# A two-layer decoder trunk on one core: the order of instructions from another model of the chip

## The chip, the core and the metric

The kernel runs on one of the eight cores of a Trainium2 chip. A core has five engines that matter here, each with its own in-order queue: PE (TensorE, matrix products), ACT (ScalarE), DVE (VectorE), POOL (GpSimd) and SP (SyncE, which here only issues loads). An engine waits at the instruction at the head of its queue until that instruction's inputs and its target buffer are free; what stands behind it waits too. The metric is the device time of one execution in microseconds.

## The reference

x holds 256 tokens of 1024 features, c one vector of 1024. Two layers follow each other, and each has three sublayers: an FFN, a mixer, an FFN. Each sublayer is

```
h = rms_norm(x, pre_g) * (1 + scale) + shift
x = x + res_w * gate * rms_norm(fn(h), post_g)
```

where shift, scale and gate come from one product of c with ada_w (1024 x 9216 per layer). The functions are:

```
swiglu: a, b = split(h @ w_in);  (silu(a) * b) @ w_out            # D_FF = 2816
hgrn2:  q, f, i, g = split(h @ w_in); a gated linear recurrence over chunks
        of 64 tokens and 8 heads; rms_norm per head, times silu(g); @ w_out
gmlp:   u, v = split(gelu(h @ w_in + b)); v = layer_norm(v)
        (u * (W_s v + b_s)) @ w_out                              # 2 x 3072 wide
```

The mixer of the first layer is hgrn2, that of the second gmlp. All data are float32.

## The kernel before

**Products.** Each float32 operand is split in two parts of the type fp32r, hi (a cast) and lo (the rest), and a product is three matmuls: hi by hi, hi by lo, lo by hi (L142 to L144 for the output product into y, L291 to L294 for the first, token-major product, L328 to L336 for the units of an FFN, L418 for the very first). The matmuls of one such group are 256 or 512 columns wide.

**Weights.** All weights pass once from HBM. `next_block` takes the blocks in a fixed list; `wblock` loads each as two halves of 128 x 1024 (tile raw, four buffers, L55), ACT casts each half to hi (L119) and DVE subtracts to get lo (L120). Twelve tiles of hi or lo exist, so six blocks; a cast has to wait until the matmuls that read the tile's former content are done. Between the weight blocks `ada` loads 144 pieces of ada_w (tile ada, two buffers), and DVE reduces each against c into a column of mod (L169, an instruction and its accumulator's readout). `pace` says how many pieces go with how many blocks. All these loads are issued by SP, and `keep_in_program_order` (L55) fixes their order to that of the code.

**Stages.** In order: ffn0 (to 207 us), HGRN2 (to 382), ffn1 (to 574), ffn2 (to 770), gMLP (to 996), ffn3 (to the end). An FFN runs through units of 256 hidden columns: two products into ups, silu on ACT, a multiplication on DVE, a split into t, and the output product of an earlier unit into four accumulators y (two token tiles t = 0, 1, each with two halves of 512 columns). The last three units' output products are left for `out_last`, which the loop at the end calls for one token tile and half after the other.

**The end of a sublayer, `tail`.** For each token tile: the output product of half 0, then ACT squares y with a row sum (L216), DVE be (L218), yg = y * G (L259); half 1, squares, root on ACT (L79, named sq), reciprocal r (L224), yg (L263), and x = x + r * yg (L265, two halves). Then `prenorm`'s part for the next sublayer: squares of x (L216), be, root, r, xn = x * r (half 0 on DVE, L233; half 1 on ACT, L235), transposes on PE into npa (L239, four per half; their banks are those of y), hf = npa * A + shift (L243, four per half on ACT), and h's hi and lo on DVE (L247, L248). The next sublayer's first product (L291) reads h. Tile 0's chain and tile 1's output product are independent of each other.

**What sets the order.** The program is written as one sequence. The framework (`tile.TileContext`) takes this sequence with the dependencies between tiles and computes from them an order for each engine, using a model of how long every instruction takes. Exceptions are marked in the code: loads stay in program order, ACT functions stay behind the table load they need (`table`, `tact`), and `after` adds an order between two instructions. Nothing else binds the order of ACT, DVE and PE beyond the dependencies.

## Time and profile before

| what | value |
|---|---|
| median of 3 runs | 1191.43 us (1189.97 to 1196.67) |
| profiled execution | 1193.24 us, of which its span 1191.5 |
| mean granted TensorE clock | 0.984 of full speed |
| weight casts L119 / subtractions L120 | 376 each, mean 1050 / 1220 ns |
| ada reductions L169 | 144, mean 1221 ns |
| bytes read from HBM | 280.11 MB, 236 GB/s over the span |

The span runs from the first to the last recorded instruction. A row of the timeline reads: start in us, busy us, engine, line, operation, output and inputs, shape, count; in brackets the idle time of the engine ahead of it and what ended it. A row of the groups reads: line, engine, operation, operands, count, then busy us and mean ns of one, then idle us before them with what ended most of it. A row of the waits reads: engine, waiting operation, what it waited for, then us in total, times and the longest.

### The profile page before, as it was taken

The numbers are of one execution on the slowest core, as the hardware profiler recorded it, in microseconds if no ns is written. First come the engines' busy times: TensorE is split into PE (matmuls) and PEld (weight loads), VectorE is DVE, ScalarE is ACT, GpSimd is POOL, SyncE is SP. The second block draws the span as 40 slices with busy tenths as digits, with TensorE's granted clock in tenths as the row PEclk, the third lists the DMA queues.
The fourth block names the chain that finished last, engine by engine and source line by source line (L and its number), as shares of the span: only waits on it lengthen the run. The fifth ranks groups of instructions, "written<-read, shape, count | busy, mean of one in ns | idle before, by whom it ended". The sixth has DMA issues, their size and how long they took to land.

```text
span 1191.5 us, 17180 instructions
## 1 busy us (share of the span) xinstructions
PE 1146.5 (96%) x6518; PEld 995.4 (84%) x6518; DVE 888.8 (75%) x1331; ACT 657.2 (55%) x1054; POOL 6.8 (1%) x16
## 2 busy tenths in 40 slices
PE   7999999997997999999999999999999999999997
PEld 6999998797895788888778888888888887888886
DVE  6997888868887887787677787657978786666652
ACT  6464446648766754456655545554754457555541
POOL 0000000000000000000000000000000000000000
PEclk9999999997999999999999999999999999999999
DMA  9899998782335777887578888537777765666640
GB/s 345 311 314 318 333 327 314 251 285 101 124 95 185 263 267 272 278 272 262 173 251 267 282 269 272 188 124 261 277 254 262 248 212 177 203 222 233 213 137 36
DMA packets 79765, 282.32 MB, mean 237 GB/s; under 512 B 9873, under 2 KB 10561, under 8 KB 79682
## 3 DMA queue, kind: packets, MB, share of 16 engines
q1 hardware_dynamic: 78626, 278.05, 68.0%
q0 software_dynamic: 1056, 3.17, 0.8%
q8 instruction: 51, 0.84, 0.3%
q14 instruction: 32, 0.26, 0.1%
HBM read 280.11 MB, written 1.07 MB: 236 GB/s over the span
## 4 chain that ended last, share of the span: by engine, by line
PE 73%; DMA 10%; DVE 8%; ACT 5%; issue 3%; SPq 0%; DVEq 0%; ACTq 0%
PE ups L328 15%; PE ups L329 8%; PE y L144 7%; PE y L142 7%; PE y L143 7%; PE ups L418 4%; DMA ada<-in_ada 4%; DMA raw<-in_wffn 4%; DVE w L120 3%; PE ups L334 3%; PE ups L336 3%; PE ups L335 3%; DMA raw<-in_whg 3%; ACT w L119 2%; PE ab L599 2%
## 5 line engine op out<-in xcount | busy, mean ns | idle before, releaser
L120 DVE TENSOR_TENSOR w<-raw,w 128x1024 fp32r<-128x1024 f32 x376 | 453.5, 1220 | 84.7 <-ACT w L119 77.5
L119 ACT CAST w<-raw 128x1024 fp32r<-128x1024 f32 x376 | 388.0, 1050 | 202.9 <-DMA raw<-in_wffn 79.4
L328 PE MATMUL ups<-h,w 128*128 128x512 f32 x864 | 303.1, 394 | 0.0
L169 DVE CUSTOM_DVE_ANT_0 junkv<-ada,cond 128x1024 bf16<-128x1024 f32 x144 | 175.8, 1221 | 92.0 <-DMA ada<-in_ada 91.5
L329 PE MATMUL ups<-h,w 128*128 128x256 f32 x864 | 242.5, 281 | 0.0
L328 PEld LDWEIGHTS ups<-h,w 128*128 128x128 f32 x864 | 162.3, 188 | 36.8
L142 PE MATMUL y<-w,t 128*128 128x512 f32 x448 | 179.4, 400 | 4.5 <-ACT t L147 4.5
L143 PE MATMUL y<-w,t 128*128 128x512 f32 x448 | 178.2, 398 | 0.0
L144 PE MATMUL y<-w,t 128*128 128x512 f32 x448 | 177.6, 397 | 0.2
L329 PEld LDWEIGHTS ups<-h,w 128*128 128x128 f32 x864 | 163.7, 190 | 0.9
L334 PE MATMUL ups<-h,w 128*128 128x256 f32 x416 | 118.3, 285 | 0.6 <-ACT w L119 0.6
L336 PE MATMUL ups<-h,w 128*128 128x256 f32 x416 | 117.8, 283 | 0.2 <-DVE w L120 0.2
L335 PE MATMUL ups<-h,w 128*128 128x256 f32 x416 | 117.6, 283 | 0.0
L142 PEld LDWEIGHTS y<-w,t 128*128 128x128 f32 x448 | 84.5, 189 | 24.1 <-ACT t L147 5.3
L144 PEld LDWEIGHTS y<-w,t 128*128 128x128 f32 x448 | 84.3, 189 | 21.0 <-DVE t L148 1.1
L143 PEld LDWEIGHTS y<-w,t 128*128 128x128 f32 x448 | 84.5, 189 | 17.9
L79 ACT ACTIVATE t<-t 128x256 f32<-128x256 f32 (+2 forms) x70 | 36.3, 523 | 97.7 <-DVE t L378 95.5
L334 PEld LDWEIGHTS ups<-h,w 128*128 128x128 f32 x416 | 79.7, 192 | 1.7 <-ACT w L119 0.8
L335 PEld LDWEIGHTS ups<-h,w 128*128 128x128 f32 x416 | 79.7, 192 | 0.8 <-issue 0.2
L336 PEld LDWEIGHTS ups<-h,w 128*128 128x128 f32 x416 | 79.7, 192 | 0.4 <-DVE w L120 0.4
L291 PE MATMUL pps<-w,h 128*128 128x512 f32 x160 | 64.4, 403 | 5.3 <-DVE h L247 5.3
L292 PE MATMUL pps<-w,h 128*128 128x512 f32 x160 | 63.8, 399 | 0.0
(199 smaller groups left out, 1435.4 us busy)
## 6 DMA issues: line engine op xcount, KB each, us to landing
raw<-in_wffn SPq DMA_DIRECT2D x264, 512.0 KB, 5.5
ada<-in_ada SPq DMA_DIRECT2D x144, 512.0 KB, 6.5
raw<-in_wgmu SPq DMA_DIRECT2D x48, 512.0 KB, 5.2
raw<-in_whg SPq DMA_DIRECT2D x40, 512.0 KB, 5.8
raw<-in_wgmv SPq DMA_DIRECT2D x24, 512.0 KB, 5.0
G<-gflat POOLq DMA_DIRECT2D x6, 512.0 KB, 5.9
t<-in_gbin SPq DMA_DIRECT2D x6, 256.0 KB, 5.2
x<-in_x SPq DMA_DIRECT2D x2, 512.0 KB, 4.0
```

What stands on the lines that cost most here:

```text
L119: nc.scalar.copy(hi[:, sl], raw)
L120: nc.vector.tensor_sub(lo[:, sl], raw, hi[:, sl])
L142: self.paced(mm(ps, l[0], r[0], start=start, stop=False))
L143: mm(ps, l[0], r[1], start=False, stop=False)
L144: mm(ps, l[1], r[0], start=False, stop=stop)
L169: nc.vector.tensor_tensor_reduce(junk, t, self.cond, 1.0, 0.0, ALU.mult, ALU.add, self.mod[i // 24][:, i % 24:i % 24 + 1])
L291: mm(res[g][t], h(0, kc), u(0, kc), start=kc == 0, stop=False)
L328: self.paced(mm(ps, u[0], self.h2[:, :, :, kc, :], start=kc == 0, stop=False))
L329: mm(ps[:, 1, :], u[1], self.h2[:, 0, :, kc, :], start=False, stop=kc == KC - 1)
L334: self.paced(mm(o, u[0], h[0], start=start, stop=False))
L335: mm(o, u[0], h[1], start=False, stop=False)
L336: mm(o, u[1], h[0], start=False, stop=stop)
```

## The change

One argument of the framework's context is set. With it the order of each engine is computed with the tool chain's timeline model, in place of its default model of an instruction's duration. No instruction, tile, buffer or load is changed, and the sequence of the code is the same.

```
--- before.py
+++ after.py
@@ -1088,7 +1088,7 @@
-    with tile.TileContext(nc) as tc:
+    with tile.TileContext(nc, schedule_with_timeline_sim=True) as tc:
         with ExitStack() as ctx:
             Body(ctx, tc, args, out).run()
```

SP's and POOL's orders are the same as before. On PE, DVE and ACT the order differs in many places. Three are shown. A name with a number is one tile: x_99 is x of tile 0 and x_100 of tile 1; `x2` is a row that comes twice.

*First place: DVE at the end of ffn0, from the update of x of tile 0 to xn.* y_799 and y_800 are the two halves of tile 1's output. Before:

```order
L265 SCALAR_TENSOR_TENSOR x_99<-yg,r,x_99 128x512 x2
L120 TENSOR_TENSOR w<-raw,w 128x1024
L218 TENSOR_SCALAR be<-s_2156 128x1
L120 TENSOR_TENSOR w<-raw,w 128x1024
L224 RECIPROCAL r<-sq 128x1
L169 ISA junkv,mod_104<-ada,cond 128x1024
L169 ISA mod_104 128x1
L233 TENSOR_SCALAR xn<-x_99,r 128x512
```

and now:

```order
L218 TENSOR_SCALAR be<-s_2156 128x1
L169 ISA junkv,mod_105<-ada,cond 128x1024
L169 ISA mod_105 128x1
L169 ISA junkv,mod_105<-ada,cond 128x1024
L169 ISA mod_105 128x1
L120 TENSOR_TENSOR w<-raw,w 128x1024 x2
L224 RECIPROCAL r<-sq 128x1
L218 TENSOR_SCALAR be<-s_2214 128x1
L259 TENSOR_TENSOR yg<-y_799,G 128x512
L120 TENSOR_TENSOR w<-raw,w 128x1024
L263 TENSOR_TENSOR yg<-y_800,G 128x512
L233 TENSOR_SCALAR xn<-x_99,r 128x512
```

Between x of tile 0 and xn there were two weight subtractions and one ada reduction; now there are three and two, and both halves of tile 1's yg, so that xn stands behind the end of y_800. After xn come, now, two more subtractions, two ada reductions and the update of x_100 ahead of the first L247; before, it was L259, an ada reduction and a subtraction.

*Second place: PE at the end of gMLP.* y_7904 and y_7905 are tile 0's halves, y_7906 and y_7907 tile 1's. Before:

```order
L142 MATMUL y_7907<-w,t_9058 128x512
L143 MATMUL y_7907<-w,t_9058 128x512
L144 MATMUL y_7907<-w,t_9058 128x512
L239 MATMUL npa<-ident,xn 128x128 x4
L142 MATMUL y_7907<-w,t_9058 128x512
L143 MATMUL y_7907<-w,t_9058 128x512
L239 MATMUL npa<-ident,xn 128x128 x4
L144 MATMUL y_7907<-w,t_9058 128x512
L142 MATMUL y_7907<-w,t_9140 128x512
```

and now:

```order
L144 MATMUL y_7906<-w,t_9161 128x512
L144 MATMUL y_7907<-w,t_9161 128x512
L142 MATMUL y_7907<-w,t_9161 128x512
L143 MATMUL y_7907<-w,t_9161 128x512
L144 MATMUL y_7907<-w,t_9161 128x512
L239 MATMUL npa<-ident,xn 128x128 x8
L291 MATMUL pps<-w,h_9339 128x512
```

Before, tile 0's y were complete some 36 matmuls before the end, and its transposes stood with 13 and 15 matmuls of tile 1 still behind them. Now the four y take turns (six matmuls each, and at the very end four each), and all eight transposes stand behind the last one. The end of HGRN2 is changed in the same manner (four y in turns, the last takes 4, 4, 4 and 7 matmuls), where transposes stood behind the last y already; at the end of ffn0 and of ffn2 the eight transposes move behind the last matmul of y.

*Third place: ACT at the end of gMLP, from the squares of y of tile 0 to the first hf.* Before:

```order
L216 ACTIVATE junka,s_9295<-y_7904 128x512
L119 CAST w<-raw 128x1024
L216 ACTIVATE junka,s_9295<-y_7905 128x512
L79 ACTIVATE sq<-s_9295,be 128x1
L216 ACTIVATE junka,s_9328<-x_99 128x512 x2
L79 ACTIVATE sq<-s_9328,be 128x1
L216 ACTIVATE junka,s_9386<-y_7906 128x512
L235 ACTIVATE xn<-x_99,r 128x512
L243 ACTIVATE hf<-npa,shift,A 128x128 x4
```

and now:

```order
L216 ACTIVATE junka,s_9295<-y_7904 128x512
L216 ACTIVATE junka,s_9295<-y_7905 128x512
L79 ACTIVATE sq<-s_9295,be 128x1
L119 CAST w<-raw 128x1024 x2
L216 ACTIVATE junka,s_9328<-x_99 128x512 x2
L216 ACTIVATE junka,s_9386<-y_7906 128x512
L216 ACTIVATE junka,s_9386<-y_7907 128x512
L79 ACTIVATE sq<-s_9328,be 128x1
L79 ACTIVATE sq<-s_9386,be 128x1
L235 ACTIVATE xn<-x_99,r 128x512
L216 ACTIVATE junka,s_9419<-x_100 128x512
L243 ACTIVATE hf<-npa,shift,A 128x128 x4
```

Two weight casts, the second square of tile 1's y with its root, and a square of x_100 have moved ahead of tile 0's hf. At the end of HGRN2 it is four casts between the root for tile 0's y and the squares of x_99.

## The prediction

> **What bounds the kernel now.** I read the page first, then PE's waits, then the timeline at each boundary between stages, and last the groups by line, for durations.
>
> ```profile
> span 1191.5 us, 17180 instructions
> PE 1146.5 (96%) x6518; PEld 995.4 (84%) x6518; DVE 888.8 (75%) x1331; ACT 657.2 (55%) x1054; POOL 6.8 (1%) x16
> PE   7999999997997999999999999999999999999997
> PEclk9999999997999999999999999999999999999999
> ```
>
> PE is busy for 1146.5 of 1191.5 us. So an order can win at most the 45 us in which PE stands still, plus what a low clock costs (the tenth and the thirteenth slice are the weak ones, about 268 to 298 and 357 to 387 us). It can lose without such a limit, wherever work that hides behind PE stops hiding. The waits of PE, as total, times and longest:
>
> ```profile
> PE pps L291 <- DVE h L247: 5.3, 5, 2.3
> PE y L142 <- ACT t L147: 4.5, 3, 2.4
> PE ots L663 <- DVE t L658: 4.4, 1, 4.4
> PE npa L239 <- DVE xn L233: 3.2, 2, 2.1
> PE fps L336 <- DVE w L120: 3.1, 2, 1.7
> PE ab L599 <- DVE t L593: 3.0, 1, 3.0
> PE ups L418 <- ACT h L950: 2.4, 1, 2.4
> ```
>
> No wait is as long as 5 us, and none lies in the repeated units of an FFN. They lie at the start, in HGRN2's elementwise part and at the boundaries. A boundary is the one place with a long chain of short steps: y of a token tile is done, then squares, root and r, x is updated, squares, root and r again, xn, transposes (npa), hf, h, first projection. The kernel before starts that chain for tile 0 while PE still works on tile 1's y. What is left uncovered shows in PE's timeline (start, busy, idle ahead in brackets), last y and then first projection or transposes, for ffn0 to HGRN2, HGRN2 to ffn1, ffn1 to ffn2, and gMLP to ffn3:
>
> ```profile
> 207.02 0.40 PE L144 MATMUL y<-w,t 128*128 128x512 f32 x1
> 209.68 0.47 PE L291 MATMUL pps<-w,h 128*128 128x512 f32 x1 [2.27 <-DVE h L247]
> ...
> 382.11 0.39 PE L144 MATMUL y<-w 128*128 128x512 f32 x1
> 383.63 1.29 PE L239 MATMUL npa<-ident,xn 128*128 128x128 f32 x8 [1.14 <-DVE xn L233]
> 386.70 0.80 PE L291 MATMUL pps<-w,h 128*128 128x512 f32 x1 [1.77 <-DVE h L247]
> ...
> 574.39 0.39 PE L142 MATMUL y<-w,t 128*128 128x512 f32 x1
> 576.83 1.84 PE L239 MATMUL npa<-ident,xn 128*128 128x128 f32 x8 [2.05 <-DVE xn L233]
> ...
> 995.56 0.40 PE L144 MATMUL y<-w,t 128*128 128x512 f32 x1
> 995.80 0.39 PE L291 MATMUL pps<-w,h 128*128 128x512 f32 x1
> ```
>
> At 995 the cover is complete: the projection follows y without a gap.
>
> **The change part by part.** Every instruction, tile and load stays, SP issues its loads in the same order, and only the sequence within PE, ACT and DVE moves. Inside an FFN casts come in other pairs, but some 20 us of matmuls per unit cover them, and no wait stands there now: I cost that at nothing. What decides is the in-order queue of ACT or DVE at a boundary: what has moved ahead of the chain delays it in full, once tile 1's y no longer covers. The durations:
>
> ```profile
> L120 DVE TENSOR_TENSOR w<-raw,w 128x1024 fp32r<-128x1024 f32 x376 | 453.5, 1220 | 84.7 <-ACT w L119 77.5 <-issue 4.5 <-PE y L143 0.9
> L119 ACT CAST w<-raw 128x1024 fp32r<-128x1024 f32 x376 | 388.0, 1050 | 202.9 <-DMA raw<-in_wffn 79.4 <-PE ups L328 28.3 <-PE y L143 20.9
> L169 DVE CUSTOM_DVE_ANT_0 junkv<-ada,cond 128x1024 bf16<-128x1024 f32 x144 | 175.8, 1221 | 92.0 <-DMA ada<-in_ada 91.5
> L265 DVE SCALAR_TENSOR_TENSOR x<-yg,r,x 128x512 f32<-128x512 f32 x24 | 17.0, 746 | 0.2
> L263 DVE TENSOR_TENSOR yg<-y,G 128x512 f32<-128x512 f32 x12 | 8.2, 686 | 14.4 <-ACT junka L216 14.2
> L216 ACT ACTIVATE junka<-y 128x512 bf16<-128x512 f32 x24 | 14.4, 598 | 39.0 <-PE y L144 38.9
> L216 ACT ACTIVATE junka<-x 128x512 bf16<-128x512 f32 x20 | 12.7, 636 | 10.3 <-DVE x L265 10.1
> L235 ACT ACTIVATE xn<-x,r 128x512 f32<-128x512 f32 x10 | 7.2, 718 | 0.3 <-DVE r L224 0.3
> L243 ACT ACTIVATE hf<-npa,shift,A 128x128 f32<-128x128 f32 x80 | 30.2, 461 | 9.9 <-DVE h L248 5.9 <-PE npa L239 3.8
> L247 DVE CAST h<-hf 128x512 fp32r<-128x512 f32 x20 | 8.5, 426 | 15.9 <-ACT hf L243 15.9
> ```
>
> *ffn0 to HGRN2: +10.* Before, DVE finished x of tile 0 by 201.4:
>
> ```profile
> 199.95 1.41 DVE L265 SCALAR_TENSOR_TENSOR x<-yg,r,x 128x512 f32<-128x512 f32 x2
> ```
>
> In the new order one ada reduction (1.3) more stands ahead of that x, and three matmuls of y_798 ahead of the last of y_797 (3 x 0.24, the step from 995.56 to 995.80), so x is there near 203.5. Between x and the first L247 DVE then has four ada reductions (4 x 1.22), five weight subtractions (5 x 1.22), L259 and L263 (0.7 each), the other half of xn (0.5), two L265 for tile 1 (1.5), and four column operations (0.6, at 0.15 each an estimate; the column root below took 0.21): 15.0, so the first L247 starts near 218.5 and ends near 219. The transposes now come after all of y_800, so PE has nothing else from 207.4. That is 219.5 for the projection against 209.68: +10. The order doesn't tell whether the last of these ada and weight blocks have landed by then (over the run DVE waits 91.5 us for ada); a late one is kept for the upper end (+15). At the lower end DVE overlaps its short steps: +7.
>
> *HGRN2 to ffn1: +10.* The four y now take turns to PE's last matmul. ACT has four casts (L119) of ffn1's weights between the root for y of tile 0 and the squares of x of tile 0, and they write blocks that the last y matmuls still read. So from the end of y (T) ACT does 4 casts (4.2), squares of x (1.3 and two readouts at 0.2, like the column root), two squares of tile 1's y (1.6), two roots (0.6), its half of xn (0.7), one square of tile 1's x (0.8), 4 hf (1.5 to 1.8, pipelined), with npa (about 0.9) between: T + 11.6 to 12; then L247 behind tile 1's two L265 and an ada, T + 14. Before it was 386.70 - 382.50 = T + 4.2. The casts alone are bounded by 4.2, the whole by 6 and 13.
>
> *gMLP to ffn3: +10.* Here too the four y are interleaved to the end: tile 0's y ends only 8 matmuls (8 x 0.23 = 1.9 us) before the last. ACT then has, behind the first root, two casts that must wait for the last matmul (2.1), squares of x (1.7), two squares of tile 1's y (1.6), two roots (0.6), half of xn (0.7), one square of tile 1's x (0.8), 4 hf (1.7), with r and npa between (1): T + 10.2, and h at T + 10.7. Before there was no gap. Lower bound: the chain without casts, about 7; upper 13.
>
> *ffn1 to ffn2, ffn2 to gMLP: +1 and +2.* Two or four casts step ahead of hf in the first, but there L243 was already the late one; in the second the transposes move behind the last y, and the bubble that opens is hf and h, 2.2 us as at 207. Bounds 0 to +3.5 and 0 to +5.
>
> *Output of HGRN2's attention (ots): +3.* Eight short squares (L645) now stand behind three and then two casts of ffn1's weights, whose data came here:
>
> ```profile
> 366.29 0.21 ACT L79 ACTIVATE ss<-ss 128x8 f32<-128x8 f32 x1
> 367.25 1.05 ACT L119 CAST w<-raw 128x1024 fp32r<-128x1024 f32 x1 [0.76 <-DMA raw<-in_wffn]
> 368.29 1.94 PE L663 MATMUL ots<-ident,t 128*128 128x128 f32 x7 [4.38 <-DVE t L658]
> 368.69 1.05 ACT L119 CAST w<-raw 128x1024 fp32r<-128x1024 f32 x1 [0.39 <-DMA raw<-in_wffn]
> ```
>
> The root at 366.29 was ahead of both and is now behind both: 369.7 instead of 366.3, so ots near 371.5, +3 (0 if the data come sooner, +4 at most).
>
> *Start: +2.* Two reductions go ahead of the first xn (2.6 on DVE) and two casts between the copies of the first transposes (2.1 on ACT); they overlap in part. Bounds 0 and +4.5:
>
> ```profile
> 15.99 4.34 PE L418 MATMUL ups<-h,w 128*128 128x256 f32 x23 [2.41 <-ACT h L950]
> ```
>
> *Gains: -2.* Some transposes of ffn1's and ffn2's first units move, so the 4.5 us of y waiting for L147 may shrink: 0 to -4. Casts ahead of HGRN2's gates and the gates' wait (L599) trade against each other: +1, with bounds of -5 and +5.
>
> *Clock: +4.* PE's granted clock is the seventh number here (us, PE, PEld, DVE, ACT, POOL, PEclk, DMA share, GB/s):
>
> ```profile
> 208.00:210.00 2.00, 0.32 (x2) 0.31 (x3) 1.66 (x3) 2.00 (x7) 0.00 (x0) 1.00 0.92 238
> 386.00:388.00 2.00, 1.30 (x3) 1.11 (x4) 1.78 (x5) 2.00 (x4) 0.00 (x0) 0.50 0.65 250
> 388.00:390.00 2.00, 2.00 (x6) 1.52 (x6) 2.00 (x4) 2.00 (x6) 0.00 (x0) 0.50 0.02 4
> 578.00:580.00 2.00, 2.00 (x8) 1.71 (x7) 1.60 (x2) 2.00 (x6) 0.00 (x0) 0.50 0.00 0
> ```
>
> After the 2.05 us at 574 the clock was half in 578 to 580 (1 lost, with the edges about 1.5); after 2.27 us at 207 it stayed full; after HGRN2 it is at half for these 4 us already. Gaps of 10 us at 207 and 995 I price like that stretch, 4 us at half, 2 lost each: +4 (0 to +7, the latter with ffn2 to gMLP and the start).
>
> [...]
>
> Sum: 10 + 10 + 10 + 1 + 2 + 3 + 2 - 2 + 1 + 4 = +41. The profiled execution took 1193.24 us (span 1191.5 and 1.7 around it), so 1234. The median is 1.8 lower: 1232.4. Once PE has stood, loads have caught up and the next casts wait less (L336's 3.1 us falls in the middle of HGRN2, after the first long gap), for which I take off 2: **1230 us**.
>
> **The rivals.** *A, partly repaid.* The pauses hit stages whose data come late: ACT waits 79.4 us for ffn weights. If loads gain during each pause, waits behind it go (fps 3.1 with 1.5 of clock as after 574, and the rest of L147's, 2.5: 7, of which 2 are in the sum), and the lower bounds of the three long tails hold (7 + 6 + 7 instead of 30): 1230 - 10 - 5 = 1215. Against it: only two ada tiles and four raw tiles can be filled, so a pause of 10 us stores little.
>
> *B, the tails also hold the loads.* A DVE queue that waits frees no ada tile and ACT's frees no raw tile, so SP stands and the following stage starves. ffn0 to HGRN2 at +15, HGRN2 to ffn1 at 13, gMLP to ffn3 at 13, ffn2 to gMLP at 5: 1230 + 5 + 3 + 3 + 3 = 1244. For it: L169 already waits 91.5 us for ada. Against it: SP's order is unchanged, and in HGRN2's tail the casts that step ahead wait for matmuls, not for data.
>
> *C, faster.* Casts of HGRN2's weights that now precede the gate chain remove the waits for weights and their half clock (L336 3.1, clock 1.5) and, with gates that come sooner, L599's 3.0; the y waits on L147 go (4.5), and ots comes no later (0 instead of +3). With that gain of 12 the kernel is faster if the tails cost less than 12 altogether; if casts there found their slots and data early enough to run while PE still works, leaving no loss, it gives 1191 - 12 = 1179. Against it: the casts behind the last y cannot run earlier, since their slots are in use.
>
> *D, no change.* PE is 96% busy and the order moves only slack, or what it loses at the tails the gains return: 1191 +- 6. For it: the seven longest waits above come to 26 of 1191 us, so nearly all matmuls stand in stages that the order can't touch. Against it: three tails in which the chain is uncovered by construction.
>
> **How the numbers follow.** The sum as worked out, 0.56; A 0.18; B 0.11; C 0.07; D 0.08. The likeliest gives 1230; its own terms, low and high ends partly compensating, about 1219 to 1242. For 8 in 10 I take 1203 to 1247: it leaves out C and most of D and a little of B's upper side. What this kernel can tell from no change is about 0.5%, 6 us (1185.5 to 1197.4). C gives faster 0.07, D gives same 0.07 and 0.01 of its edge goes to slower; all others slower, 0.86.
>
> **What would show it.** In the changed profile: PE idle of about 10 us between the last y and the first L291 at 207, 383 and 996, released by DVE h L247, with weight casts or ada reductions next to it on ACT and DVE; ots waiting near 7; ffn units unchanged in length; PE busy near 1150. It would be wrong if those gaps stay under 4 us, if a wait of PE on weights inside ffn2 or ffn3 appears (B), or if the HGRN2 stage from first projection to ots is shorter by more than 5 us (C).

## The result, and the profile after

The changed kernel took 1268.82 us (median of 4 runs, 1265.34 to 1270.71) against 1193.13 us for the kernel before: a ratio of 1.0639, with a 95% interval of 1.0612 to 1.0667. It is slower by 76 us, where 37 to 39 us were forecast, and above the range's end of 1247. The page of the profiled execution (1270.71 us, its span 1268.9):

```profile
span 1268.9 us, 17271 instructions
PE 1164.0 (92%) x6518; PEld 1009.8 (80%) x6518; DVE 890.1 (70%) x1331; ACT 664.0 (52%) x1054; POOL 6.8 (1%) x16
PEclk9999998998987899999899999999899997999999
```

DVE and ACT do the same work in nearly the same time, 890 us against 889 and 664 against 657. PE loses in two ways, which together are the 77.4 us by which the span grew. It stands still for 105.0 us instead of 45.0, which is 60.0 more. And its 6518 matmuls are busy for 1164.0 us instead of 1146.5, which is 17.5 more, at a mean granted clock of 0.961 instead of 0.984. Its waits (what waited, for what: total, times, longest):

```profile
PE npa L239 <- ACT xn L235: 19.7, 3, 13.0
PE pps L291 <- DVE h L247: 17.5, 7, 5.2
PE y L142 <- ACT t L147: 7.6, 4, 3.0
PE ots L663 <- DVE t L658: 7.5, 1, 7.5
PE ups L328 <- DVE t L378: 7.3, 3, 4.4
PE npa L239 <- DVE xn L233: 6.7, 2, 6.1
PE vps L854 <- ACT w L852: 6.1, 1, 6.1
...
PE vps L854 <- DVE t L861: 3.3, 3, 2.1
```

The waits of transposes and first projections (npa, pps) for xn and h came to 10 us before (5.3, 3.2 and 1.7) and come to 44 now. But ups (for L378) and vps, which lie inside stages, have entries too, where 0 and 1.6 us stood before. PE's timeline shows both parts. Of each boundary the last y and the first L291, of the changed kernel, with the rows between them left out (but for the transposes at HGRN2's end):

```profile
209.22 0.40 PE L144 MATMUL y<-w,t 128*128 128x512 f32 x1
222.21 0.77 PE L291 MATMUL pps<-w,h 128*128 128x512 f32 x1 [5.23 <-DVE h L247]
391.37 0.39 PE L144 MATMUL y<-w 128*128 128x512 f32 x1
404.77 1.11 PE L239 MATMUL npa<-ident,xn 128*128 128x128 f32 x4 [13.02 <-ACT xn L235]
410.29 0.79 PE L291 MATMUL pps<-w,h 128*128 128x512 f32 x1 [2.64 <-DVE h L247]
609.27 0.39 PE L144 MATMUL y<-w,t 128*128 128x512 f32 x1
615.83 0.76 PE L291 MATMUL pps<-w,h 128*128 128x512 f32 x1 [3.75 <-DVE h L247]
816.84 0.40 PE L144 MATMUL y<-w,t 128*128 128x512 f32 x1
820.03 0.47 PE L291 MATMUL pps<-w,h 128*128 128x512 f32 x1 [1.92 <-DVE r L224]
1059.57 0.40 PE L144 MATMUL y<-w,t 128*128 128x512 f32 x1
1069.39 0.77 PE L291 MATMUL pps<-w,h 128*128 128x512 f32 x1 [1.40 <-DVE h L247]
1262.27 0.40 PE L144 MATMUL y<-w,t 128*128 128x512 f32 x1
```

and those of the kernel before that the prediction does not show:

```profile
581.69 0.40 PE L144 MATMUL y<-w,t 128*128 128x512 f32 x1
581.93 0.39 PE L291 MATMUL pps<-w,h 128*128 128x512 f32 x1
774.79 0.40 PE L144 MATMUL y<-w,t 128*128 128x512 f32 x1
775.02 0.40 PE L291 MATMUL pps<-w,h 128*128 128x512 f32 x1
1184.79 0.40 PE L144 MATMUL y<-w,t 128*128 128x512 f32 x1
```

The differences of these starts divide each span without a rest (us; "to" is a boundary, from the last y to the first L291; a stage runs from there to its last y):

| piece | before | changed | more |
|---|---|---|---|
| start and ffn0 | 207.0 | 209.2 | +2.2 |
| ffn0 to HGRN2 | 2.7 | 13.0 | +10.3 |
| HGRN2 | 172.4 | 169.2 | -3.3 |
| HGRN2 to ffn1 | 4.6 | 18.9 | +14.3 |
| ffn1 | 195.0 | 199.0 | +4.0 |
| ffn1 to ffn2 | 0.2 | 6.6 | +6.3 |
| ffn2 | 192.9 | 201.0 | +8.1 |
| ffn2 to gMLP | 0.2 | 3.2 | +3.0 |
| gMLP | 220.5 | 239.5 | +19.0 |
| gMLP to ffn3 | 0.2 | 9.8 | +9.6 |
| ffn3 and end | 195.7 | 199.5 | +3.8 |

The five boundaries cost 43.5 us, the insides of the stages 33.9. How far such a row can be trusted shows in the runs below that leave a stage's order as it was: there ffn1 took 191 to 196 us and once 200, ffn2 189 to 194, gMLP 220.5 to 222 and ffn3 195.7 to 198.3. So the 4 us of ffn1 and of ffn3 say little, ffn2's 8 and gMLP's 19 say much.

### The profile page after: what moved, and what is told of

Same layout as the page of the kernel before. It is cut to its first block, busy times and chain, and to the rows that moved or that the text cites. A ratio compares the mean times of both kernels' runs of the same rounds, so it can differ in the third digit from the quotient of the medians.

```text
span 1268.9 us, 17271 instructions
## 1 busy us (share of the span) xinstructions
PE 1164.0 (92%) x6518; PEld 1009.8 (80%) x6518; DVE 890.1 (70%) x1331; ACT 664.0 (52%) x1054; POOL 6.8 (1%) x16
## 4 chain that ended last, share of the span: by engine, by line
PE 61%; DMA 18%; DVE 12%; issue 4%; ACT 4%; SPq 1%; DVEq 0%; ACTq 0%
DMA ada<-in_ada 12%; PE ups L328 12%; DVE w L120 7%; PE ups L329 6%; PE y L142 5%; PE y L143 5%; PE y L144 5%; DMA raw<-in_wffn 5%; PE ups L418 4%; PE ups L336 3%; PE ups L334 3%; PE ups L335 3%; PE pps L291 3%; PE pps L292 2%; PE pps L294 2%
## 5 line engine op out<-in xcount | busy, mean ns | idle before, releaser
L119 ACT CAST w<-raw 128x1024 fp32r<-128x1024 f32 x376 | 385.6, 1050 | 277.9 <-DMA raw<-in_wffn 127.4
L328 PE MATMUL ups<-h,w 128*128 128x512 f32 x864 | 308.6, 400 | 8.4 <-DVE t L378 7.3
L169 DVE CUSTOM_DVE_ANT_0 junkv<-ada,cond 128x1024 bf16<-128x1024 f32 x144 | 176.0, 1222 | 127.8 <-DMA ada<-in_ada 127.4
L329 PE MATMUL ups<-h,w 128*128 128x256 f32 x864 | 243.7, 282 | 0.0
L328 PEld LDWEIGHTS ups<-h,w 128*128 128x128 f32 x864 | 164.3, 190 | 48.3 <-DVE t L378 8.3
L329 PEld LDWEIGHTS ups<-h,w 128*128 128x128 f32 x864 | 165.3, 191 | 1.1
L334 PE MATMUL ups<-h,w 128*128 128x256 f32 x416 | 120.7, 290 | 0.0
L336 PE MATMUL ups<-h,w 128*128 128x256 f32 x416 | 119.4, 287 | 0.0
L335 PE MATMUL ups<-h,w 128*128 128x256 f32 x416 | 119.3, 287 | 0.0
L143 PEld LDWEIGHTS y<-w,t 128*128 128x128 f32 x448 | 84.6, 189 | 18.9 <-DVE w L120 0.5
L291 PE MATMUL pps<-w,h 128*128 128x512 f32 x160 | 68.9, 434 | 19.5 <-DVE h L247 17.5
L334 PEld LDWEIGHTS ups<-h,w 128*128 128x128 f32 x416 | 81.6, 196 | 1.0 <-issue 0.2
L335 PEld LDWEIGHTS ups<-h,w 128*128 128x128 f32 x416 | 81.5, 196 | 0.9 <-issue 0.2
L336 PEld LDWEIGHTS ups<-h,w 128*128 128x128 f32 x416 | 81.3, 195 | 0.3
L292 PE MATMUL pps<-w,h 128*128 128x512 f32 x160 | 67.9, 424 | 0.0
```

What stands on the lines that cost most here:

```text
L119: nc.scalar.copy(hi[:, sl], raw)
L143: mm(ps, l[0], r[1], start=False, stop=False)
L169: nc.vector.tensor_tensor_reduce(junk, t, self.cond, 1.0, 0.0, ALU.mult, ALU.add, self.mod[i // 24][:, i % 24:i % 24 + 1])
L291: mm(res[g][t], h(0, kc), u(0, kc), start=kc == 0, stop=False)
L328: self.paced(mm(ps, u[0], self.h2[:, :, :, kc, :], start=kc == 0, stop=False))
L329: mm(ps[:, 1, :], u[1], self.h2[:, 0, :, kc, :], start=False, stop=kc == KC - 1)
```

## The experiments

All but the last three are orders. The program is the changed kernel's, and a table at its end fixes the order of PE, ACT and DVE by dependencies between neighbours that wait for nothing:

```
     with tile.TileContext(nc, schedule_with_timeline_sim=True) as tc:
         with ExitStack() as ctx:
             Body(ctx, tc, args, out).run()
+            force(nc, tc)
...
+for n in table_of_the_engine:
+    if prev is not None:
+        tc.add_manual_dep(ins[n], prev, <NoSync>, reason="issue order")
+    prev = ins[n]
```

A table that joins the two orders takes one up to a named instruction and what the other has left from there. Where such a table only follows the order before, its stage lengths above and below agree with the kernel before (206.6 to 206.9 us for ffn0), so the table itself costs nothing that shows.

**Where is the loss?** First the tails against the rest.

```
-changed: all
+changed to the middle of ffn0; before to fps; changed to the last chunk's
+gate (L593); before to ffn1's first unit; changed to the end of gMLP;
+before to ffn3's first unit; changed to the end
```

> The changed kernel's order, but from the middle of ffn0 to HGRN2's first unit (fps), from HGRN2's last chunk to ffn1's first unit, and from the end of gMLP to ffn3's first unit the order of before. Theory (each tail loses on its own, for what stands ahead of its chain): these three stretches lost 12 + 20 + 11 us between the two profiles, so 1269 - 43 = 1226 us. Rival (the lateness only shows at the tails, and comes from loads that are late over whole stages): little is won there or it is lost again in the next stage, 1245 us or more.

Measured: 1224.31 us, 1.0271 of before (1.0242 to 1.0299). And the complement, the same cuts with the two orders exchanged:

```
-before: all
+before to the middle of ffn0; changed to fps; before to the last chunk's gate;
+changed to ffn1's first unit; before to the end of gMLP;
+changed to ffn3's first unit; before to the end
```

> The complement: the order of before, but in the same three stretches that of the changed kernel. Theory: 1193 + 43 = 1236 us. Rival: the tails cost little when the stages around them run with the old order, 1215 us or less.

Measured: 1235.94 us, 1.0353 (1.0317 to 1.0389). Both are what was expected within 2 us. The tails cost 42.8 us on their own, and taking them out of the changed kernel wins 44.5; the rest costs 31.2 on its own, and 42.8 + 31.2 = 74.0 of the 75.7. The two parts add up, so neither is a consequence of the other.

```
-before: all
+before to fps; changed to the last chunk's gate; before to the end
```

> The order of before, but from HGRN2's first unit (fps) to its last chunk that of the changed kernel, where the changed kernel was 8 us quicker. Theory (the new order there removes the waits for weight casts, L334 and L336, and starts L599 earlier): 1193 - 7 = 1186 us. Rival (it is only repayment: the stop ahead of that stage let the loads run ahead): 1193 us within 3.

Measured: 1189.49 us, 0.9979 (0.9955 to 1.0004). Its HGRN2 took 167.5 us instead of 172.4, as the theory of a real gain wants, but the time cannot be told from no change.

```
-before: all
+before to gMLP's first unit (L334); changed to the end of gMLP; before to the end
```

> The order of before, but from gMLP's first unit (L334) to the end of gMLP that of the changed kernel, where it lost some 17 us. Theory (the new order itself makes the layer norm's product, vps, and the unit's products wait): 1193 + 17 = 1210 us. Rival (it was late there because the loads were behind after the stages before): 1200 us or less.

Measured: 1206.78 us, 1.0126 (1.0103 to 1.0149): gMLP's loss is of the order there (its stage took 237.9 us), and not lateness brought along from the stages ahead.

**Which engine?** Exchanging ACT's or DVE's order alone is not possible, since the engines would wait for each other in a circle. In PE's order of before, tile 0's transposes stand ahead of tile 1's last matmuls of y; in the new orders DVE at the end of ffn0, and ACT at the end of gMLP, reach tile 0's xn only behind a step that reads that finished y. PE's order alone can be exchanged:

```
-PE: before     ACT: before   DVE: before
+PE: changed    ACT: before   DVE: before
```

> PE's order of the changed kernel over the whole program, ACT and DVE in the order of before. Theory (PE's order costs only the cover of the chains: 2 at the end of ffn0, 6 at the end of HGRN2, 8 at the end of gMLP, 2 at the end of ffn2): 1193 + 18 = 1211 us. Rival (PE's order is the cause, and ACT's and DVE's follow from it): 1235 us or more. Rival (the waits ahead of PE are all from ACT and DVE): 1193 within 6.

Measured: 1245.14 us, 1.0453 (1.0423 to 1.0482): the second reading, and not mine. PE's order alone loses 54 us (1191.43 was measured beside it), but not in the same places: HGRN2 takes 190.2 us, 18 more than before, where the changed kernel is 3 us shorter; the boundaries cost 26.1 instead of 51.5. PE in a new order waits for steps that ACT and DVE then take in the old one:

```profile
PE pps L291 <- DVE h L247: 12.2, 7, 3.2
PE npa L239 <- DVE xn L233: 10.9, 4, 4.3
PE ab L599 <- DVE t L593: 10.6, 3, 5.3
```

So the 54 us are no share of the 76: three orders that don't belong together have a price of their own. What the run does show, boundary by boundary, is what PE's new place for y and the transposes suffices for: 4.5 us at ffn0's end (13.0 with all three), 8.3 at HGRN2's (18.9), 7.4 at gMLP's (9.8).

**What holds the chains?** By the prediction, casts and reductions ahead of the chain's own steps. So they were all put behind, in the changed kernel (ACT at the end of HGRN2, as an example):

```
 L79 ACTIVATE sq<-s_3780,be 128x1
-L119 CAST w<-raw 128x1024 x4
 L216 ACTIVATE junka,s_3807<-x_99 128x512 x2
...
 L243 ACTIVATE hf<-npa,shift,A 128x128 x4
+L119 CAST w<-raw 128x1024 x4
```

> The changed kernel's order, but in the five tails, from the first half's square (L216, L259) to tile 0's first hf (L243) on ACT and first L247 on DVE, the weight casts, subtractions and ada reductions stand behind the chain's own steps; PE keeps the new order. Theory (what stands ahead of the chain costs its time and its waits): some 9 us at the end of ffn0, 8 at the end of HGRN2, 3 at the end of gMLP and 2 elsewhere less than 1269: 1247 us. Rival (the loss is the cover that PE's new order gives up, the casts would only have run elsewhere): 1260 us or more.

Measured: 1293.47 us, 1.085 (1.0818 to 1.0882), 24.7 slower than the changed kernel. The boundaries do what the theory wants (5.2 us at ffn0's end instead of 13.0, 9.6 at HGRN2's instead of 18.9), and the stages behind them give back more: HGRN2 takes 191.0 us and ffn1 214.4. The edit was a poor one: at ffn0's end it put some twenty rows of loads' work in one block on DVE between the hi part of h's first half (L247, at 213.9 us) and its lo part (L248, at 236.8). The same edit on the order of before, together with HGRN2's middle:

```
-L119 CAST w<-raw 128x1024
-L119 CAST w<-raw 128x1024 x2
-L119 CAST w<-raw 128x1024
 L243 ACTIVATE hf<-npa,shift,A 128x128 x4
+L119 CAST w<-raw 128x1024 x4
```

> The order of before, with HGRN2's middle in the new order and with the casts, subtractions and ada reductions of the five tails behind the chain's own steps. Theory (what waits in the tails of before is the same kind: the 2.3 us ahead of the first projection at 207 and some 2 us elsewhere go, and HGRN2's 3 us): 1193 - 6 = 1187 us. Rival (what is moved behind is then late for the next stage): 1193 us or more.

Measured: 1207.42 us, 1.0126 (1.01 to 1.0152): 1.1 us at ffn0's end instead of 2.7, and HGRN2 at 183.8 us. A cleaner cut, then: in the run with the new tails, at the end of HGRN2 only, and behind both tiles' h.

```
 L79 ACTIVATE sq<-s_3780,be 128x1
-L119 CAST w<-raw 128x1024 x4
 L216 ACTIVATE junka,s_3807<-x_99 128x512 x2
...
 L243 ACTIVATE hf<-npa,shift,A 128x128 x12
+L119 CAST w<-raw 128x1024 x4
 L79 ACTIVATE t_4057<-pps 128x512
```

> As the run with the order of before and the three new tails (1235.9 us), but at the end of HGRN2 the four casts (L119) behind the root, their subtractions and the three ada reductions (L120, L169) stand behind the last hf and h of both token tiles. They are needed some 30 us later. Theory (the casts cost the chain their 4.2 us and the 2.2 and 3.1 us for which they waited for data in that run's trace): 1236 - 9 = 1227 us. Rival (as in the run with all loads last, what is moved behind holds something later for as long): 1233 us or more.

Measured: 1240.76 us, 1.0405 (1.0372 to 1.0438). The boundary falls from 19.4 to 11.8 us, 7.6 of the 9 expected, and ffn1 rises from 195.6 to 208.7. Where it went is PE's longest wait between 380 and 480 us of that run, for a split behind six casts of later weights (in the next run's trace the last two of the six wait 1.70 and 3.35 us for their data):

```profile
PE y L142 <- ACT t L147: 9.1, 1, 9.1
```

So that split was put ahead of the casts too:

```
 L79 ACTIVATE t_4057<-pps 128x512
+L147 CAST t_4055<-tps 128x2x128
+L147 CAST t_4056<-tps 128x2x128
 L119 CAST w<-raw 128x1024 x4
 L79 ACTIVATE t_4069<-pps 128x512
-L119 CAST w<-raw 128x1024 x2
-L147 CAST t_4055<-tps 128x2x128
```

> As the run with HGRN2's end and the four casts moved back (1240.8 us), but ffn1's first activation, the split of the first transposed tile (L147 on ACT, L393 and L148 on DVE) also stand ahead of the next weight casts and subtractions; in that run PE's y waited 9.1 us for this L147, which stood behind eight casts. Theory Q (a chain waits for what stands ahead of it in its queue, data included): the 9 us come back, 1232 us. Theory S (the stream of weights is what is late, since casts that are held hold the raw tiles and so the loads; PE's new order needs a block before it can go on): the wait turns into one of y or ups for weights, 1238 us or more.

Measured: 1244.57 us, 1.0441 (1.0422 to 1.0461), and the same stretch shows:

```profile
PE tps L396 <- DVE t L393: 9.4, 2, 4.9
PE y L142 <- ACT w L119: 8.3, 1, 8.3
```

The wait for the split has become one for a weight block: y's first matmuls of ffn1 stand ahead of the second transposes (four of them here; two in PE's order of before), and they need the next block. Whoever holds the casts back holds back that block. This is theory S's prediction. Inside gMLP the same happened twice. First the column steps of v's norm ahead of the casts, in a window that was too wide (36 rows of loads' work on DVE):

```
 L79 ACTIVATE t_8031<-ups,gbinu 128x256 x2
-L119 CAST w<-raw 128x1024 x5
 L852 ACTIVATE w<-w,nm,rr 128x512 x6
-L119 CAST w<-raw 128x1024
+L119 CAST w<-raw 128x1024 x8
 L852 ACTIVATE w<-w,nm,rr 128x512 x6
```

> As the run with gMLP alone in the new order (1206.8 us), but the casts, subtractions and ada reductions between v's last statistics (L830) and its normalisation (L834 on DVE, L852 on ACT) stand behind these steps. Theory (the column steps of the norm, threaded between casts that wait for their data, hold the product vps 7.6 us): 1199 us. Rival (the casts are late anyhow, and the units then wait for weights): 1205 us or more.

Measured: 1216.63 us, 1.0194 (1.0158 to 1.0229), worse than without the edit. Then with ten rows on DVE, and on ACT the same difference:

> As the run with gMLP alone in the new order (1206.8 us), but the ten subtractions and ada reductions between v's last statistics (L806) and the end of its norm's column steps (L834) on DVE, and the seven casts around the first normalisations (L852) on ACT, stand behind these steps: a narrower edit than the one that gave 1216.6. Theory (the product vps then starts some 7 us earlier and nothing else is late): 1199 us. Rival (the units' next weights come that much later instead): 1206 us or more.

Measured: 1207.34 us, 1.0124 (1.0094 to 1.0153), no gain. The first six L852 start at 846.7 us instead of 856.9, but PE then waits for the second six, which now start at 865.5 us instead of 862.1, behind casts that wait 1.92, 2.70, 1.61 and 0.15 us for data. No run put both groups of six ahead of the casts, so whether the norm's place on ACT is what gMLP loses by was not tested to the end. Rows of PE and ACT of this run:

```profile
860.73 1.04 ACT L119 CAST w<-raw 128x1024 fp32r<-128x1024 f32 x1 [2.70 <-DMA raw<-in_wgmu]
...
865.54 4.34 ACT L852 ACTIVATE w<-w,nm,rr 128x512 f32<-128x512 f32 x6
866.40 1.65 PE L854 MATMUL vps<-w 128*128 128x128 f32 x6 [6.82 <-ACT w L852]
```

**And the ada reductions?** In ffn1's and ffn2's units of the changed kernel, on DVE:

```
 L378 TENSOR_TENSOR t_4113<-t_4113,ups 128x256
 L148 TENSOR_TENSOR t_4056<-tps,t_4056 128x2x128
-L169 ISA junkv,mod_105<-ada,cond 128x1024
-L169 ISA mod_105 128x1
 L382 TENSOR_TENSOR t_4114<-t_4114,ups 128x256
+L169 ISA junkv,mod_105<-ada,cond 128x1024
+L169 ISA mod_105 128x1
```

> The changed kernel's order, but in ffn1's and ffn2's units the ada reductions on DVE stand one or two of the unit's own steps (L378, L382, L384, L148) later; 53 of them move. Theory (a reduction that waits for its load holds L378, and with it ACT and PE: L328 waited 7.3 us for L378, most of it in these two stages): 1269 - 6 = 1263 us. Rival (the units' waits come from the casts on ACT): 1268 us within 3.

Measured: 1258.05 us, 1.0547 (1.0513 to 1.0581), 10.8 us less than the changed kernel. ffn2 takes 193.3 us instead of 201.0; ffn1's 194.5 instead of 199.0 is within what it varies by. The groups by line, the changed kernel's and this run's (behind the bar: busy, mean ns, idle ahead and for what):

```profile
L169 DVE CUSTOM_DVE_ANT_0 junkv<-ada,cond 128x1024 bf16<-128x1024 f32 x144 | 176.0, 1222 | 127.8 <-DMA ada<-in_ada 127.4
```

```profile
L169 DVE CUSTOM_DVE_ANT_0 junkv<-ada,cond 128x1024 bf16<-128x1024 f32 x144 | 175.6, 1219 | 70.0 <-DMA ada<-in_ada 69.5
```

In gMLP, by the same edit on the run with gMLP alone in the new order:

```
-L169 ISA junkv,mod_108<-ada,cond 128x1024
-L169 ISA mod_108 128x1
 L834 SCALAR_TENSOR_TENSOR nm<-mv,rr 128x1
 L95 SCALAR_TENSOR_TENSOR rs_q<-rs_y,rs_hv 128x1
+L169 ISA junkv,mod_108<-ada,cond 128x1024
+L169 ISA mod_108 128x1
```

> As the run with gMLP alone in the new order (1206.8 us), but 14 ada reductions on DVE in gMLP's units and gate stand two of the other steps later. DVE waited 23.3 us for ada there, against 9.3 with the old order. Theory Q (as in the FFN units, where the same edit won 11 us): 1201 us. Theory S (gMLP is late for weights, whatever stands ahead): 1206 us within 3.

Measured: 1207.45 us, 1.0138 (1.0115 to 1.0161), no gain. So gMLP's loss does not hang on ada.

**Queue or stream?** Three runs take the ada loads out of the matter; none of them computes the product of c with ada_w, so only their times count. The first has the changed order, without DVE's wait:

```
-            nc.vector.tensor_tensor_reduce(junk, t, self.cond, 1.0, 0.0, ALU.mult, ALU.add,
+            nc.vector.tensor_tensor_reduce(junk, self.cond, self.cond, 1.0, 0.0, ALU.mult, ALU.add,
```

> The changed kernel with its whole order, but the ada reductions on DVE read c's own tile instead of the loaded piece of ada_w, so they wait for no load (shift, scale and gate are then not the reference's); the loads themselves stay in full. DVE waited 127 us for ada. Theory Q (the loss in the units and in part of the tails is DVE's queue waiting for ada): 1269 - 30 = 1239 us. Theory S (the stream of loads is what is late, the casts then wait as long): 1260 us or more.

Measured: 1242.91 us, 1.0437 (1.041 to 1.0465): 25.9 us less than the changed kernel, near theory Q's 30 and not within theory S's bound. It does not part the two theories cleanly, though. With no reader of the ada tiles, SP is free of them too: in the changed kernel it waited 57.4 us for DVE's L169 before it could issue a load, and here L169 reads none of their tiles. ACT's casts, which the edit does not touch, wait 81.4 us for ffn weights instead of 127.4. The second moves fewer bytes as well:

```
-            self.load(t, self.d["ada"][i])
+            self.load(t[:, 0:64], self.d["ada"][i][:, 0:64])
```

> As that run, and each ada load brings 64 of its 1024 columns, so that 71 of 278 MB are not moved; the number and order of loads stay. Theory Q: as that run within 4, since nothing waits for ada any more. Theory S: the weights come sooner by what the ada loads took, 1235 us or less even if the run before is at 1260.

Measured: 1241.32 us, 1.0429 (1.0403 to 1.0456), the same within the spread: a quarter of the bytes less wins nothing once no queue waits for them. The casts' waits for ffn weights fall once more, from 81.4 to 45.3 us, and the time stays. As a matter of bytes, theory S falls. The third has both edits with the order of before:

> The order of before with the same two edits (64 columns of each ada load, reductions that read c's tile). PE was busy 96% of the span, so at most the waits for ada at the tails go: 1186 us, and both theories want it within 8 of 1193. The distance to the run before says what the new order costs without the ada loads: by Q some 45 us (the tails' casts and PE's cover), by S 35 or less.

Measured: 1172.55 us, 0.9858 (0.9825 to 0.989). Neither theory had that: the ada loads cost the kernel before 18 us, where I had allowed 8. The distance between the last two runs is 68.8 us, against the 45 and 35 expected, and 75.7 with the ada loads. By pieces the new order still costs 38.9 us at the boundaries and 29.8 inside, of which gMLP 15.8 (234.8 against 219.0) and ffn2 2.3 (191.0 against 188.7). So waiting for ada explains most of ffn2's loss (8.1 before), and little of the boundaries' (43.5) and of gMLP's (19.0).

**A version that beats both?** Two tables on the order of before. HGRN2's first half alone:

```
-before: all
+before to fps; changed to the second chunk's gate (L593); before to the end
```

> The order of before, but from HGRN2's first unit to its second chunk's gates (some 70 us) that of the changed kernel; the run with the new order up to the last chunk was 7 us ahead in its trace there and kept 1 at the end. Theory (the gain is made before the first L599 and lost where the two orders are joined later): 1193 - 6 = 1187 us. Rival (a gain ahead of HGRN2's own chain of chunks is waited away at its end): 1190 us or more.

Measured: 1189.41 us, 0.9989 (0.9967 to 1.0012), no difference. And that with single casts behind the chains:

```
 L235 ACTIVATE xn<-x_99,r 128x512
-L119 CAST w<-raw 128x1024
 L243 ACTIVATE hf<-npa,shift,A 128x128 x4
+L119 CAST w<-raw 128x1024
```

> The order of before with HGRN2's first half in the new order (1189.4 us) and, at the ends of ffn0, HGRN2, ffn1 and gMLP, the one to three casts, subtractions and ada reductions that stood directly ahead of the first hf or h put behind them: five casts, seven on DVE. Theory Q: some 1.5 us at each of two ends and 1 at a third, 1185 us. Theory S (given back in the next stage): 1189 us within 3.

Measured: 1194.76 us, 1.0015 (0.9995 to 1.0034). The boundaries fall from 8.0 to 5.5 us, and the stages take it back. No order run here beats that of before by more than can be told from no change.

## Why the prediction was wrong

The direction was right, and so was the reading that the loss sits at the boundaries, as far as it went: 43.5 us there against 33 in the terms. The step that failed is "Inside an FFN casts come in other pairs, but some 20 us of matmuls per unit cover them, and no wait stands there now: I cost that at nothing", and that gMLP's inside had no term at all. Those insides lost 33.9 us, where my terms (start, ots, HGRN2 and the gains) come to 4. The clock was mis-sized as well: PE's longer matmuls are 17.5 us where the term is 4, and PE's standing is 60.0 where all other terms come to 37. PE's busy time was one of the signs named, "near 1150", and it is 1164.0.

*ffn0 to HGRN2, +10: right, +10.3, with two sizes off that cancel in part.* DVE's queue is the one that was added up. DVE of the changed kernel, from x of tile 0 to the first L247:

```profile
203.93 1.41 DVE L265 SCALAR_TENSOR_TENSOR x<-yg,r,x 128x512 f32<-128x512 f32 x2
206.51 1.23 DVE L169 CUSTOM_DVE_ANT_0 junkv<-ada,cond 128x1024 bf16<-128x1024 f32 x1 [0.89 <-DMA ada<-in_ada]
209.37 1.23 DVE L169 CUSTOM_DVE_ANT_0 junkv<-ada,cond 128x1024 bf16<-128x1024 f32 x1 [1.62 <-DMA ada<-in_ada]
221.64 0.42 DVE L247 CAST h<-hf 128x512 fp32r<-128x512 f32 x1
```

x was done at 205.3 (203.93 + 1.41; 203.5 forecast), as the whole stage ended 2.2 us later, and the first L247 started at 221.6 (218.5 forecast). Of the 16.3 us between, 2.5 are two waits for ada, the ones kept "for the upper end", and 13.8 are work, where 15.0 had been added up.

*HGRN2 to ffn1, +10: short by 4.* The mechanism was right, and the mis-sized term is "4 casts (4.2)". ACT there:

```profile
391.56 1.99 ACT L119 CAST w<-raw 128x1024 fp32r<-128x1024 f32 x2 [0.45 <-PE y L143]
395.72 1.05 ACT L119 CAST w<-raw 128x1024 fp32r<-128x1024 f32 x1 [2.16 <-DMA raw<-in_wffn]
399.12 1.05 ACT L119 CAST w<-raw 128x1024 fp32r<-128x1024 f32 x1 [2.36 <-DMA raw<-in_wffn]
404.00 0.72 ACT L235 ACTIVATE xn<-x,r 128x512 f32<-128x512 f32 x1 [0.64 <-DVE r L224]
```

The last two casts wait 4.5 us for data: their duration was counted, and the wait that each carries with it was not. That ran through the whole prediction. ACT's casts waited 79.4 us for ffn weights before, and 127.4 now; DVE's reductions 91.5 us for ada, and 127.4. I quoted the first two numbers for the rivals A and B and for an upper bound, and put none of it into the sum. (The durations that I added up to "T + 11.6 to 12" come to 12.0 to 12.3, which is small beside it.)

*gMLP to ffn3, +10: right, +9.6*, and by the run with PE's order alone 7.2 us of it (7.4 against 0.2) are the cover that PE gives up, near the lower bound of 7 that was named for it.

*ffn1 to ffn2, +1: wrong, +6.3.* I read the row at 574 as the end of y. It was the end of tile 0's part; tile 1's y went on to 581.69 and covered the rest of the chain. (The stage ends 574 and 770 given above are of this kind; by the last y they are 582 and 775.) With the transposes behind all y, that cover is gone; PE's order alone gives 3.0 there. DVE's new order adds four weight subtractions ahead of the first h (609.83 to 614.70 us), which no term held. *ffn2 to gMLP, +2: +3.0. ots, +3: +3.1* (7.50 against 4.38 us of waiting). *Start, +2: +2.2.* The wait of the very first transposes (xps for xn), which the prediction's list of waits leaves out, grew from 3.6 to 5.7 us.

*Gains, -2, and HGRN2, +1.* L147's waits grew from 4.5 to 7.6 us. HGRN2 from its first L291 to its last y became 3.3 us shorter even with ots' 3 in it: the waits for L336 are gone and PE waits 2.0 instead of 3.0 us at L599, a gain that I had given to rival C. L336 is what the 2 us taken off at the end of the sum had counted on; over the whole run, though, ACT's casts waited longer for ffn weights, not less.

*FFN units, 0: +8 in ffn2, up to +4 in ffn1.* DVE's queue at the end of ffn2 shows it, with ACT and PE behind it:

```profile
765.11 1.23 DVE L169 CUSTOM_DVE_ANT_0 junkv<-ada,cond 128x1024 bf16<-128x1024 f32 x1 [3.68 <-DMA ada<-in_ada]
767.39 0.42 DVE L378 TENSOR_TENSOR t<-t,ups 128x256 f32<-128x256 f32 x1
767.85 0.42 ACT L79 ACTIVATE t<-t 128x256 f32<-128x256 f32 x1 [2.82 <-DVE t L378]
767.87 0.67 PE L328 MATMUL ups<-h,w 128*128 128x512 f32 x1 [4.43 <-DVE t L378]
```

The reduction waits for its load, L378 stands behind it, the accumulator is not freed, and PE stops. The 20 us of cover are no protection where a step waits for data ahead of it in an in-order queue. Moving these reductions by one or two steps won 10.8 us, 7.7 of them in ffn2, which shows it there.

*gMLP: +19, without a term.* That it is the order there is shown (1206.78 us alone). PE's busy time in that stage divides the loss, before and then changed (us of the stage, then busy us of PE, PEld, DVE, ACT and POOL, then the clock):

```profile
775.02:995.56 220.54, 218.13 (x1269) 189.29 (x1268) 169.11 (x266) 119.99 (x176) 1.07 (x2) 1.00 0.68 231
820.03:1059.57 239.54, 223.32 (x1260) 194.81 (x1261) 167.22 (x255) 118.93 (x162) 1.08 (x2) 0.97 0.62 215
```

PE stands 16.2 us instead of 2.4, and its matmuls take 5.2 longer. What in the order does it is not settled. The trace names the casts that wait for data ahead of the norm (0.90, 1.47, 1.00 and 1.58 us between 898 and 907, then vps for L852, 6.1 us, and behind it a clock of 0.50 from 908 to 914), a second wait of vps for L861 (3.3 against 1.6) and y's waits for L147 (1.1 and 3.0, where gMLP had none), but no single edit won it back: not the first normalisations earlier, not the ada reductions later, not ada away altogether. PE's order alone makes gMLP 10.0 us longer (230.5 against 220.5). I hold that PE's, ACT's and DVE's new orders there lean on each other, which is argued from that and from the edit's second wait, and not shown.

*Clock, +4: 17.5 by PE's busy time.* At the boundaries it was as expected in kind. Windows behind three of them (the seventh number is the granted clock):

```profile
414.00:416.00 2.00, 2.00 (x7) 1.52 (x6) 0.80 (x2) 0.00 (x0) 0.00 (x0) 0.50 0.00 0
823.00:825.00 2.00, 2.00 (x11) 1.65 (x10) 1.28 (x4) 1.95 (x4) 0.00 (x0) 1.00 0.03 10
1069.00:1071.00 2.00, 1.60 (x4) 1.36 (x5) 1.50 (x4) 1.95 (x4) 0.00 (x0) 0.50 0.03 8
1073.00:1075.00 2.00, 2.00 (x6) 1.62 (x5) 0.70 (x2) 0.16 (x1) 0.00 (x0) 0.50 0.00 0
```

Half the clock for some 6 us behind the gap at 1060 (0.50 from 1069 to 1075), so by estimate 3 lost and not 2; of ffn3's +3.8 that is most, though this row varies by nearly as much. What the term did not hold are half clocks inside the stages, behind waits that it had at nothing (in gMLP 0.50 from 908 to 914 behind the 6.1 us for L852, and 0.50 in 1048 to 1050 behind 3.0 us for L147): gMLP's matmuls alone took the 5.2 us above. Behind the 3.2 us from ffn2 to gMLP, with one wait of 1.92 us in them, the clock stayed full (1.00 in 823 to 825); behind the 2.05 us at 574 in the kernel before it had not (0.50 in 578 to 580).

*The rivals.* B had a part of what happened, that queues wait for loads, but put its cause at the tails alone and its price at 14 us; its sign, a wait of PE on weights inside ffn2, appears with 1.2 us. A is refuted: nothing was repaid, since the two halves add up to 74.0 of 75.7. C's gain exists in HGRN2's length, with 3 to 5 us, and could not be told from nothing in the kernel's time (1189.49 us).

What stays open is the common cause behind the edits that moved a chain and won nothing. The bytes of ada are excluded (1242.91 against 1241.32 us). Waiting for ada is shown for ffn2 and excluded as the main part for gMLP and the boundaries. Of the remaining 69 us, 39 are at the boundaries, where the chains of the prediction stand uncovered, and 30 inside the stages. That these lie in how the three orders fit each other, with casts standing where their data are late, is what the wait for a weight block behind the moved split and the run with PE's order alone point to; it is not shown.

## What to carry to other kernels

An instruction that is moved ahead in an in-order queue brings the wait for its data with it (2.16 and 2.36 us ahead of two casts of 1.05 at HGRN2's end), so its duration is the least to count for it. The mean wait of its line is a first estimate of the rest, and not a safe one: four reductions at 0.64 us each (91.5 us over 144) give 2.5 at ffn0's end, where 2.5 were measured, but four casts at 0.3 each (79.4 us over the 264 of ffn weights) give 1.2 at HGRN2's end, where 4.5 were. That no wait shows in a stage now says nothing about an order that puts loads' work at another place in that stage: walk through each stage's queues, and not only those where PE waits today. And where an edit frees one chain, look at the time and not at the chain: here five such edits moved the chain as wanted, and a later place gave it back.

## What the runs showed that was not expected

The ada loads cost the kernel before 18 us (1172.55 against 1190.91) although PE was busy 96% of its span and none of its longest waits names them. In the trace 11.7 us of that are PE standing (45.0 against 33.3) and 9.0 are shorter matmuls (1146.5 against 1137.5). In the changed order the same two edits win 27.5 us, of which the 71 MB that are not moved count for 1.6, inside the spread of the runs.

Tables that fix the orders can join two schedules at a point in time at no cost that shows, as the runs by stretches did. Joining them by engine is another matter: PE's order of the changed kernel over ACT's and DVE's of before made HGRN2 190.2 us long, where the two matched sets take 172.4 and 169.2.
